# Narrower first scores and last weighed keys in the attention of a streaming-encoder block

## The chip, the cores and the metric

The kernel runs on one core of a Trainium2 chip. The metric is the device time of one execution in microseconds. TensorE is called PE here, its weight loads PEld, VectorE DVE, ScalarE ACT, GpSimd POOL, and SyncE, which issues most loads, SP.

## The reference, cut to what matters

One layer works on 512 frames of 1024 features. Most of its work is projections; the change is in the attention, with 16 heads of 64 features.

```python
xn = rmsnorm(h, norm_mix_g[l])
u = jnp.einsum('bsd,de->bse', xn, w_in[l])
q, k, v, xr, gr, ga, gb = jnp.split(u, splits, axis=-1)
ya = chunked_band_attention(q, k, v, rel_table[l]) @ w_attn_out[l]
...                       # recurrent branch yb, gates g_a and g_b
h = h + (g_a * ya + g_b * yb) @ w_o[l]
...                       # SwiGLU feed-forward, final norm
# in the attention: chunks of 64 frames, each sees its own chunk and 8 before it
s = jnp.einsum('bnqhd,bnkhd->bhnqk', q, kb).astype(jnp.float32) * scale
s = s + rel_bias_band(rel_table)
s = jnp.where(valid, s, NEG_INF)
p = jax.nn.softmax(s, axis=-1)
o = jnp.einsum('bhnqk,bnkhd->bnqhd', p, vb)
```

With 512 frames there are 8 chunks, so a frame sees every key up to the end of its own chunk: the scores are block-triangular.

## The kernel before, in words

All products run on PE with operands of the type fp32r, a 32-bit type that carries fewer bits of the mantissa. To reach fp32 accuracy each operand is split into a high part and a low rest: ACT copies a tile to fp32r (line 80) and DVE subtracts that from the original (line 81). A projection then multiplies three times for each block of 128 features (lines 74 to 76: high by high, high by low, low by high).

The stages follow each other: norm and recurrent branch with its projections, attention, the output projections, the feed-forward block. The attention stage lies in the profile from about 235 to 449 us. For each head:

- `scores(h)` makes four score tiles, one for each block `qb` of 128 queries. Block `qb` needs the first `(qb + 1) * 128` keys. The matmul's stationary operand is a block of q, the moving operand the keys `kh` and then `kl` (lines 624 and 625). The tiles of `qb` 0, 1 and 3 share two PSUM buffers with the tag `s`; that of `qb` 2 takes one of the four `mm` buffers. DVE adds the bias and finds the maximum (627), ACT makes the exponential and its row sum (628), DVE takes the reciprocal of the sums (629), POOL scales (631).
- `transposed(h, prob)` turns the ten 128x128 blocks on PE into three PSUM tiles (643), and each is split into `pp[0]`, `pp[1]`, `pp[2]`. The third holds key block 2 (two query blocks) and key block 3 (one).
- `weigh(h, pp)` multiplies with v into one PSUM tile `o` (663): key block by key block, high and low. The halves of the result are then summed by ACT (664) and DVE (665) into `oacc`.

Both places that the change touches work with at least 256 columns in the moving operand. Query block 0 computes 256 key columns of which 128 are read. Key block 3 is weighed with 256 columns, the first 128 of which POOL has filled with zeros (637), so that the third tile has a gap at columns 256 to 383, and its split is made in two pieces.

Between the heads the projections of q and k for the next pair of heads, of v, and of the gate run as fill: a list of steps of which `fill` takes some before and some after each weighing. `k_tile` copies the high part of k twice (584 and 586), subtracts on DVE (585), and POOL copies the rest (587); the scores of a new pair's first head need these. The order of instructions on each engine is not the program's own: a scheduler of the framework (`schedule_with_timeline_sim=True`) places all instructions by its model of their costs, so a change of one operation can move others. Each engine works through its instructions in the order so made.

## Time and profile before

| what | value |
|---|---|
| median of three runs | 892.38 us (891.75 to 892.43) |
| the profiled execution | 892.82 us |
| its span in the profile | 891.0 us |
| granted PE clock | 0.996 of full speed |
| PE busy | 875.7 us, 98% |
| DVE, ACT, POOL busy | 553.5, 473.2, 130.2 us |

The rows that follow have a start, a length, an engine, a source line, an operation and the tiles as "output<-inputs", with the sizes of the operands. In a group's row the count stands behind an x, then the busy time, the mean of one in ns, the idle time of the engine just before these instructions, and what ended that idle time. Matmuls overlap and their ends are modelled, so the cost of a matmul is read from the distance of two starts and not from its length.

### The profile page before, as it was taken

To read this page: it belongs to the slowest core of one execution; us is meant where nothing else is said; L and a number is where in the kernel's file an instruction comes from. 1 tells how busy PE (TensorE), PEld (TensorE's weight loads), DVE (VectorE), ACT (ScalarE), POOL (GpSimd) and SP (SyncE) were. 2 spreads that over 40 slices of the span, in tenths; PEclk is the share of its full clock that TensorE was granted. 3 is DMA by queue.
4 is the path that set the end of the run, shared out by engine and by line. 5 is a ranking of instruction groups with operands and counts; after the bars stand their busy time and mean duration, and the time that the engine had idled before them with its cause. 6 is when DMAs were issued, how large, how long until landed. Compare 5 with 4: busy or idle time off the path is not lost.

```text
span 891.0 us, 13319 instructions
## 1 busy us (share of the span) xinstructions
PE 875.7 (98%) x5220; PEld 779.4 (87%) x5220; DVE 553.5 (62%) x863; ACT 473.2 (53%) x841; POOL 130.2 (15%) x168
## 2 busy tenths in 40 slices
PE   8999999999999999999999999899999999999997
PEld 5988888888889889898888889899999999888886
DVE  5777557563466675666456356998788887463203
ACT  7566646652266676667434366556655556723203
POOL 4012112120022222323000003400000001300200
PEclk9999999999999999999999999899999999999999
DMA  8323223333332232331224430333333333253102
GB/s 264 89 79 111 82 91 95 120 95 95 106 104 74 77 101 72 94 96 61 71 85 145 172 95 25 95 119 116 122 95 95 97 115 101 97 187 125 37 1 96
DMA packets 85024, 89.06 MB, mean 100 GB/s; under 512 B 5344, under 2 KB 73552, under 8 KB 84960
## 3 DMA queue, kind: packets, MB, share of 16 engines
q1 hardware_dynamic: 83584, 84.73, 30.7%
q10 hardware_dynamic: 1376, 3.47, 1.0%
q8 instruction: 41, 0.67, 0.3%
q14 instruction: 23, 0.19, 0.1%
HBM read 86.05 MB, written 2.14 MB: 99 GB/s over the span
## 4 chain that ended last, share of the span: by engine, by line
PE 94%; DVE 3%; ACT 1%; issue 1%; DMA 1%; POOL 0%; SPq 0%; ACTq 0%
PE po_out L74 5%; PE po_out L76 5%; PE po_out L75 5%; PE p_fu L75 2%; PE p_fu L74 2%; PE o L663 2%; PE p_fu L76 2%; PE p_fg L75 2%; PE p_fg L76 2%; PE p_fg L74 2%; PE pT L643 2%; PE po_v L76 2%; PE po_v L75 2%; PE po_v L74 2%; PE po_q L74 2%; PE q_fg L76 2%
## 5 line engine op out<-in xcount | busy, mean ns | idle before, releaser
L75 PE MATMUL po_out<-whl_fo,act_hi 128*128 128x512 f32 (+1 forms) x198 | 72.4, 366 | 0.0
L74 PE MATMUL po_out<-whl_fo,act_hi 128*128 128x512 f32 (+1 forms) x198 | 72.4, 366 | 0.0
L76 PE MATMUL po_out<-whl_fo,act_lo 128*128 128x512 f32 (+1 forms) x198 | 71.6, 365 | 0.0
L631 POOL TENSOR_SCALAR p<-p,rl 128x128 f32<-128x128 f32 (+1 forms) x64 | 35.9, 583 | 142.0 <-DVE rl L629 142.0
L81 DVE TENSOR_TENSOR whl_fo<-raw_fo,whl_fo 128x1024 fp32r<-128x1024 f32 x22 | 27.6, 1261 | 45.5 <-ACT whl_fo L80 45.1
L80 ACT ACTIVATE whl_fo<-raw_fo 128x1024 fp32r<-128x1024 f32 x22 | 22.9, 1056 | 49.3 <-PE po_out L76 35.0
L627 DVE CUSTOM_DVE_ANT_0 p<-s,bias 128x384 f32<-128x384 f32 (+2 forms) x64 | 29.5, 484 | 21.5 <-PE s L625 20.9
L76 PEld LDWEIGHTS po_out<-whl_fo,act_lo 128*128 128x128 f32 x198 | 37.3, 189 | 6.0
L75 PEld LDWEIGHTS po_out<-whl_fo,act_hi 128*128 128x128 f32 x198 | 37.4, 189 | 6.0
L74 PEld LDWEIGHTS po_out<-whl_fo,act_hi 128*128 128x128 f32 x198 | 37.4, 189 | 6.0
L628 ACT ACTIVATE p<-p,m 128x384 f32<-128x384 f32 (+2 forms) x64 | 35.7, 560 | 12.6 <-DVE m L627 12.2
L843 POOL TENSOR_TENSOR act_lo<-act,act_hi 128x1024 fp32r<-128x1024 f32 x4 | 10.5, 2621 | 185.9 <-ACT act_hi L842 184.4
L76 PE MATMUL po_v<-whl_v,xnT 128*128 128x256 f32 x128 | 36.2, 283 | 0.0
L75 PE MATMUL po_v<-whl_v,xnT 128*128 128x256 f32 x128 | 36.1, 282 | 0.0
L74 PE MATMUL po_v<-whl_v,xnT 128*128 128x256 f32 x128 | 36.1, 282 | 0.0
L81 DVE TENSOR_TENSOR pp<-pT,pp 128x512 fp32r<-128x512 f32 (+1 forms) x64 | 29.3, 484 | 5.3 <-ACT pp L80 5.0
L81 DVE TENSOR_TENSOR whl_fu_s<-s_fu,whl_fu_s 128x1024 fp32r<-128x1024 f32 x20 | 25.3, 1280 | 5.8 <-ACT whl_fu_s L80 5.7
L75 PE MATMUL po_xr<-xnT,whl_xr 128*128 128x512 f32 (+1 forms) x80 | 27.9, 354 | 0.6 <-DVE xnT L331 0.6
L74 PE MATMUL po_gr<-xnT,whl_gr 128*128 128x512 f32 (+1 forms) x80 | 27.8, 349 | 0.1
L76 PE MATMUL po_gr<-xnT,whl_gr 128*128 128x512 f32 (+1 forms) x80 | 27.5, 348 | 0.3 <-DVE whl_gr L81 0.3
L75 PE MATMUL po_gr<-xnT,whl_gr 128*128 128x512 f32 (+1 forms) x80 | 27.6, 346 | 0.0
L74 PE MATMUL po_xr<-xnT,whl_xr 128*128 128x512 f32 (+1 forms) x80 | 26.6, 351 | 0.8 <-ACT xnT L330 0.8
(354 smaller groups left out, 3077.1 us busy)
## 6 DMA issues: line engine op xcount, KB each, us to landing
raw_fg<-in_w_ffn_in_dram SPq DMA_DIRECT2D x22, 512.0 KB, 4.4
raw_fu<-in_w_ffn_in_dram SPq DMA_DIRECT2D x22, 512.0 KB, 3.5
raw_fo<-in_w_ffn_out_dram SPq DMA_DIRECT2D x22, 512.0 KB, 4.0
raw_qk<-in_w_in_dram SPq DMA_DIRECT2D x32, 256.0 KB, 3.2
raw_xr<-in_w_in_dram SPq DMA_DIRECT2D x8, 512.0 KB, 4.6
raw_gr<-in_w_in_dram SPq DMA_DIRECT2D x8, 512.0 KB, 3.5
raw_ga<-in_w_in_dram SPq DMA_DIRECT2D x8, 512.0 KB, 3.9
raw_gb<-in_w_in_dram SPq DMA_DIRECT2D x8, 512.0 KB, 3.5
```

Source lines behind the costliest of these rows:

```text
L74: pe.matmul(o, sh, mh, start=start, stop=False, skip_group_check=parts)
L75: pe.matmul(o, sh, ml, start=False, stop=False, skip_group_check=parts)
L76: pe.matmul(o, sl, mh, start=False, stop=stop, skip_group_check=parts)
L80: act.activation(hi, src, AF.Copy)
L81: dve.tensor_sub(lo, src, f(hi))
L627: dve.tensor_tensor_reduce(prob[qb][:], sc[:, 0:w], bias[:, S - w:S], -1.0, 3e38, ALU.add, ALU.min, nmax[:, qb:qb + 1])
L628: act.activation(prob[qb][:], prob[qb][:], AF.Exp, bias=nmax[:, qb:qb + 1], scale=-1.0, accum_out=lsum[:, qb:qb + 1])
L631: pool.tensor_scalar(prob[qb][:], prob[qb][:], rl[:, qb:qb + 1], 1.0, ALU.mult, ALU.mult)
L643: pe.transpose(pt[:, at * P:(at + 1) * P], prob[qb][:, kb * P:(kb + 1) * P], ident[:])
L663: pe.matmul(po[:, S - n:S], st, pp[i][:, part, lo:lo + n], start=kb == 0 and part == 0, stop=kb == NT - 1 and part == 1)
L843: (pool if i in (0, 1, 2, 4) else dve).tensor_sub(lo[:], o[:], f(hi[:]))
```

## The change

Three edits, all in the attention.

- The scores of query block 0 are made for 128 key columns, where there were 256. The other blocks keep their widths.
- The third transpose tile is split in one piece of 384 columns, so key block 3 now lies at columns 256 to 383 of `pp[2]`; the gap, and POOL's zero fill of it, go.
- Key block 3 is weighed with 128 columns into the last 128 columns of `o`, where there were 256 into the last 256.

The third transposes stay in a bank of the four `mm` buffers, as they are before.

```diff
         for qb in range(NT):
             w = (qb + 1) * P
-            wm = max(w, 256)
...
-            pe.matmul(sc[:, 0:wm], qs, kh[:, e, 0:wm], start=True, stop=False)
-            pe.matmul(sc[:, 0:wm], qs, kl[:, e, 0:wm], start=False, stop=True)
+            pe.matmul(sc[:, 0:w], qs, kh[:, e, 0:w], start=True, stop=False)
+            pe.matmul(sc[:, 0:w], qs, kl[:, e, 0:w], start=False, stop=True)
...
         pp = [aw2.tile([P, 2, S], F32R, tag="pt", bufs=4, name=f"pp{h}_{i}") for i in range(3)]
-        pool.memset(f(pp[2][:, :, 256:384]), 0.0)
...
-            for at, lo, n in (((0, 0, 512),), ((0, 0, 384),), ((0, 0, 256), (384, 256, 128)))[i]:
-                split(pp[i][:, 0, at:at + n], pp[i][:, 1, at:at + n], pt[:, lo:lo + n])
+            n = (512, 384, 384)[i]
+            split(pp[i][:, 0, 0:n], pp[i][:, 1, 0:n], pt[:, 0:n])
...
-            i, lo, n = ((0, 0, 512), (1, 0, 384), (2, 0, 256), (2, 256, 256))[kb]
+            i, lo, n = ((0, 0, 512), (1, 0, 384), (2, 0, 256), (2, 256, 128))[kb]
```

In the changed kernel the lines from 624 on carry numbers that are one lower, and from 638 on two lower.

## The prediction

> **What bounds the kernel now.** I read the page first, then the stretches of the attention stage, then PE's own timeline there, then the order in which the built instructions of both kernels stand on each engine.

> ```profile
> span 891.0 us, 13319 instructions
> PE 875.7 (98%) x5220; PEld 779.4 (87%) x5220; DVE 553.5 (62%) x863; ACT 473.2 (53%) x841; POOL 130.2 (15%) x168
> ...
> PE 94%; DVE 3%; ACT 1%; issue 1%; DMA 1%; POOL 0%; SPq 0%; ACTq 0%
> ...
> 300.00:325.00 25.00, 24.51 (x126) 20.80 (x125) 16.02 (x34) 16.28 (x35) 7.23 (x14) 1.00 0.32 86
> ```

> PE is busy for 98% of the span and makes 94% of the chain that ended last. The last row is one stretch of the attention stage (length, then busy time of PE, weight loads, DVE, ACT, POOL, granted clock 1.00): PE has half a microsecond free in 25, the others a third of their time or more. So only two things can move the time: what a PE instruction costs, and how long PE waits. Work taken from ACT, DVE and POOL counts only through waits of PE.

> **What a matmul costs.** Starts of neighbouring matmuls and weight loads give the pace.

> ```profile
> 235.83 0.28 PE L624 MATMUL s<-kh,q 128*128 128x256 f32 x1
> 235.95 0.28 PE L625 MATMUL s<-kl,q 128*128 128x256 f32 x1
> 236.07 0.34 PE L624 MATMUL s<-kh,q 128*128 128x384 f32 x1
> 236.25 0.34 PE L625 MATMUL s<-kl,q 128*128 128x384 f32 x1
> 236.42 0.39 PE L74 MATMUL po_yb<-rnn,whl_yb 128*128 128x512 f32 x1
> 236.65 0.40 PE L75 MATMUL po_yb<-rnn,whl_yb 128*128 128x512 f32 x1
> ...
> 9.72 0.30 PEld L74 LDWEIGHTS po_xr<-xnT,whl_xr 128*128 128x128 f32 x2 [0.65 <-ACT xnT L330]
> 10.27 0.19 PEld L75 LDWEIGHTS po_xr<-xnT,whl_xr 128*128 128x128 f32 x1 [0.25 <-DVE xnT L331]
> 10.38 0.19 PEld L76 LDWEIGHTS po_xr<-xnT,whl_xr 128*128 128x128 f32 x1
> ...
> 302.97 1.09 PE pT L643 x10
> ```

> The next matmul starts 0.12 us after one of 256 columns, 0.17 to 0.18 after 384, 0.23 after 512: about 0.053 for each 128 columns, and 0.012 on top. A matmul of 128 columns would by that line take 0.053 + 0.012, some 0.065. But every one of these matmuls brings its own weights. Two loads that follow each other after a pause, with no full matmul between them to set the pace, stand 0.11 apart (10.27 and 10.38; and two in 0.30 where one takes 0.19). I read 0.11 as the least distance of two loads, so a narrow matmul can hardly pass in less. The only matmuls of 128 columns in this stage, the transposes, also go at 0.109 each (10 in 1.09, from the chain).

> **The change part by part.** First, the narrowed matmuls.

> ```profile
> L624 PE MATMUL s<-kh,q 128*128 128x256 f32 x32 | 9.7, 325 | 2.0 <-ACT kh L586 2.0
> ...
> L625 PE MATMUL s<-kl,q 128*128 128x256 f32 x32 | 8.5, 294 | 0.0
> ...
> L663 PE MATMUL o<-pp,v 128*128 128x256 f32 x64 | 11.7, 281 | 0.0
> ```

> Half of each group is narrowed (block 0 of the two score blocks of that width, key block 3 of the two in the weighing): 16 + 16 + 32 = 64 matmuls. At 0.12 before and 0.11 after I take 0.01 each, **-0.6 us**. No row shows a product of this type with fewer than 256 columns, so both ends stay open: at 0.065 the 64 save 0.055 each, -3.5 us; if such a product needed four passes it would cost what 512 columns cost, 0.23, or +0.11 each, +7.0 us. I take 0.11 because the load rows and the transposes both lie there.

> [...]

> Second, what leaves the other engines: 16 zero fills on POOL, and one split in place of two for each third transpose tile.

> ```profile
> L637 POOL MEMSET pp<- 128x256 f32 x15 | 4.8, 318 | 8.3 <-PE o L663 7.6
> ...
> L80 ACT ACTIVATE pp<-pT 128x384 fp32r<-128x384 f32 x16 | 7.7, 482 | 0.0
> ...
> L80 ACT ACTIVATE pp<-pT 128x256 fp32r<-128x256 f32 x16 | 6.2, 386 | 0.0
> L80 ACT ACTIVATE pp<-pT 128x128 fp32r<-128x128 f32 x16 | 4.4, 275 | 1.5 <-DVE pp L81 1.3
> ```

> ACT has 386 + 275 - 482 = 179 ns less for each head, 2.9 us in all, DVE about as much, POOL some 5 us. PE's busy time hides all of that; I cost it at nothing by itself. If that cover were gone, at most 0.18 us per head, 2.9 us, could show as gain.

> Third, the order. A scheduler places the instructions, and 16 fewer operations make it place them anew. The built order of PE is nearly as before until head 4; then it differs in many places of the attention stage, and behind that stage it is the same again. SP only swaps a load with its neighbour twice; the weight copies that read such loads keep PE waiting nowhere in the rows here, so that is nothing. Most moves are neutral: a transpose or a weighing slipped into a projection. One is not, and it comes twice, at heads 6 and 14. Before, PE goes: all of the last k projection, 8 weighing matmuls of head 4, 10 transposes of head 5, then the first scores of head 6, which need the new k. These rows are that place:

> ```profile
> 309.96 0.39 PE L76 MATMUL po_k<-xnT,whl_qk 128*128 128x512 f32 x1
> 310.18 1.44 PE L663 MATMUL o<-pp,v 128*128 128x512 f32 x8
> 311.46 1.25 PE L643 MATMUL pT<-ident,p 128*128 128x128 f32 x10
> 313.21 0.68 PE L624 MATMUL s<-kh,q 128*128 128x256 f32 x3 [0.49 <-ACT kh L586]
> ...
> 310.38 0.59 ACT L584 ACTIVATE kh<-po_k 64x512 fp32r<-64x512 f32 x1 [1.60 <-PE po_k L76]
> 310.88 1.05 ACT L80 ACTIVATE whl_v<-raw_v 128x1024 fp32r<-128x1024 f32 x1
> 311.95 0.59 ACT L664 ACTIVATE oacc<-o 64x512 f32<-64x512 f32 x1
> 312.57 0.59 ACT L586 ACTIVATE kh<-po_k 64x512 fp32r<-64x512 f32 x1
> 313.18 0.59 ACT L584 ACTIVATE kh<-po_k 64x512 fp32r<-64x512 f32 x1
> ...
> 311.96 1.48 DVE L81 TENSOR_TENSOR whl_v<-raw_v,whl_v 128x1024 fp32r<-128x1024 f32 x1 [0.27 <-ACT whl_v L80]
> 313.36 0.67 DVE L665 TENSOR_TENSOR oacc<-o,oacc 64x512 f32<-64x512 f32 x1
> 314.07 0.70 DVE L585 TENSOR_TENSOR kl<-po_k,kh 64x512 fp32r<-64x512 f32 x1
> ...
> L628 ACT ACTIVATE p<-p,m 128x512 f32<-128x512 f32 x16 | 11.6, 724 | 10.0 <-DVE m L627 10.0
> ...
> L627 DVE CUSTOM_DVE_ANT_0 p<-s,bias 128x128 f32<-128x128 f32 x16 | 4.5, 283 | 2.2 <-PE s L625 1.8
> ```

> The scores wait for ACT's second copy of kh, which ends at 313.16. PE was done with its transposes at 311.46 + 1.09 = 312.55 and waits 0.66. In the changed order two things are otherwise. The last score block of head 5 stands inside the k projection, three matmuls from its end, so its exponential (724 ns; neighbours on ACT overlap by some 0.09, as 310.38 + 0.59 against 310.88 shows) falls between the weight copy at 310.88 and the oacc copy: the kh copy ends 0.63 later, at 313.8. And the scores stand ahead of the ten transposes, so PE is at them at 310.18 + 1.28 = 311.46 and waits until 313.84, with the 1.09 of transposes still to do. That is 0.63 + 1.09 = 1.72 us lost each time.

> Behind it follows a second wait. After two score blocks and three transposes (0.46 + 0.33, to 314.63) PE wants the 512-column block of head 6, whose PSUM buffer is free when DVE has read block 0. On DVE that read stands behind the second kl subtraction, which needs the fifth row of ACT: that copy follows the kh copy from 313.8 to 314.4, then 0.70 and 0.28 on DVE, to about 315.4. PE waits 0.77. Queued behind it are the rest of head 5's transposes and the next projection. Together 2.5 us each time, **+5.0 us** for two. Bounds: 1.1 each (the exponential finds a gap on ACT and the buffer comes free in time, so only the 1.09 of transposes is lost) to 2.6 (a restart costs 0.1 more), so 2.2 to 5.2.

> Fourth, a gain at the end of the stage.

> ```profile
> PEld pT L643 <- POOL p L631: 0.7, 2, 0.4
> ```

> These two waits of the last head's transposes for POOL's scaling have more projection ahead of the chain they wait for in the new order, and POOL is 5 us lighter: I take **-0.7**, bounds 0 and -0.7.

> Sum: 5.0 - 0.6 - 0.7 = **+3.7 us**. The profiled execution took 892.82 with a span of 891.0, so 1.8 lie around the span; the median of the three runs is 892.38, 0.4 less. On the median I forecast 892.4 + 3.7 = **896.1 us**. No change can be told below 0.2%, 1.8 us, either way.

> **Rivals.** (1) Four passes: the narrow products cost as much as 512 columns, +7.0 instead of -0.6. The narrow weighings just ahead of the two long waits would be hidden in them (four times 0.11, 0.4 us): 892.4 + 5.0 + 7.0 - 0.4 - 0.7 = 903.3. For it speaks only that no narrow product of this type is in the trace; against it the transposes, also 32-bit, at 0.109. (2) Streaming pace: narrow products at 0.065, -3.5: 892.4 + 5.0 - 3.5 - 0.7 = 893.2, no change to be told. Against it speak the loads 0.11 apart. [...] (3) The new waits do not come: ACT runs ahead at heads 6 and 14 so that the waits stay what they were: 892.4 - 0.6 - 0.7 = 891.1. Against it: nothing lies between 310.38 and 313.16 on ACT but its own work, and one more operation stands in that row. (4) Faster: loads overlap more than the rows show, narrow products go at 0.065, and the freed 0.18 us per head on ACT covers the new waits: 892.4 - 3.5 - 0.7 = 888.2. It decides where the narrow interval is under 0.10 (64 times 0.02 and the 0.7 make 1.9) and the waits at both places stay at what they are now.

> **How the numbers follow.** My forecast has 0.70, with a range of its own from 893.3 (waits at 2.2) to 897.6 (waits at 5.2, the two gains at nothing). Four passes 0.11, streaming pace 0.09, no new waits 0.04, faster 0.06. From 891.0 to 898.2 the range takes the forecast with some room for restart costs, and rivals 2 and 3; rivals 1 and 4 and a tail of 0.02 are left out. Slower by over 0.2%: 0.68 of the forecast and 0.11, 0.79. Within: 0.09 + 0.04 + 0.02 = 0.15. Faster: 0.06.

> **What would show it.** In PE's timeline after, narrow scores and weighings follow each other by 0.11; 0.065 or 0.23 would prove rival 2 or 1. In the waits, scores on ACT's kh come four times as now, but two of them with some 2.4 us, and new waits of scores on DVE's read of p, two with some 0.8. If PE's idle time in the stage from the first scores to the last weighing does not grow by 4 to 5 us, the third step is wrong, whatever the total.

## The result: 1% slower, two and a half times what was forecast

| | us |
|---|---|
| before, median of 4 | 892.15 |
| the changed kernel, median of 4 | 901.31 (899.84 to 902.49) |
| ratio, 95% interval | 1.0102 (1.0083 to 1.0122) |
| forecast, range | 896.1 (891.0 to 898.2) |

The change costs 9.2 us, where +3.7 was forecast, and lies outside the range. The sign and the two places are as forecast; the size is not. The profiled execution of the changed kernel took 899.84, 7.0 more than that of before (892.82), and was the shortest of the four.

From the page of the changed kernel, its span and the first two engines:

```profile
span 898.1 us, 13316 instructions
PE 876.3 (98%) x5220; PEld 779.8 (87%) x5220; DVE 554.0 (62%) x847; ACT 472.5 (53%) x825; POOL 123.5 (14%) x152
```

PE still has 98% of the span, and its busy time hardly moved (875.7 before), so the loss must be sought in single stretches. The next view cuts the trace at the two places that the prediction named. Columns: stretch, length, then busy time (and count) of PE, weight loads, DVE, ACT, POOL, then the granted clock, the DMA share and GB/s. First the changed kernel, then before:

```profile
308.00:326.00 18.00, 14.02 (x67) 11.55 (x66) 9.67 (x24) 9.40 (x22) 5.63 (x12) 0.91 0.34 88
408.00:426.00 18.00, 14.98 (x68) 12.39 (x67) 10.35 (x25) 10.61 (x24) 5.49 (x11) 0.91 0.23 73
426.00:500.00 74.00, 74.00 (x348) 61.89 (x347) 41.77 (x60) 30.05 (x45) 2.06 (x4) 1.00 0.30 102
```

```profile
308.00:326.00 18.00, 17.51 (x90) 14.83 (x89) 11.78 (x24) 12.10 (x24) 7.23 (x14) 1.00 0.33 88
408.00:426.00 18.00, 17.50 (x95) 14.93 (x94) 10.19 (x21) 11.67 (x24) 5.55 (x11) 1.00 0.20 61
426.00:500.00 74.00, 73.79 (x338) 61.12 (x337) 41.35 (x60) 29.29 (x46) 2.05 (x4) 1.00 0.39 135
```

Two things changed in each place. PE's idle time went from 0.49 to 3.98 and from 0.50 to 3.02 us: 6.0 more in all. And the granted clock, 1.00 before, is 0.91 over 18 us. The second was in no step of the prediction and in no rival. (The granted clock is the share of the full clock that PE was given; 0.50 is half clock.)

PE's timeline at head 6 in the changed kernel (start, length, line, tiles; in brackets the idle time ahead and what ended it):

```profile
309.43 0.39 PE L76 MATMUL po_k<-xnT,whl_qk 128*128 128x512 f32 x1
309.66 1.37 PE L661 MATMUL o<-pp,v 128*128 128x512 f32 x8
313.38 0.50 PE L623 MATMUL s<-kh,q 128*128 128x128 f32 x2 [2.36 <-ACT kh L586]
313.72 0.39 PE L624 MATMUL s<-kl,q 128*128 128x128 f32 x2
315.73 1.14 PE L641 MATMUL pT<-ident,p 128*128 128x128 f32 x3 [1.62 <-POOL p L630]
316.52 0.78 PE L623 MATMUL s<-kh,q 128*128 128x512 f32 x1
```

The weighings come at once behind the k projection; then PE waits 2.36 us for ACT's second copy of kh, makes four short score matmuls, and waits a second time, 1.62 us, for POOL. At head 14 the same two waits take 2.36 and 0.53. What follows is stretched: from the first of three transposes to the next start it is 0.79, 0.26 each, where the prediction's rows had 0.109. The chain of copies on ACT there:

```profile
309.86 0.59 ACT L584 ACTIVATE kh<-po_k 64x512 fp32r<-64x512 f32 x1 [2.11 <-PE po_k L76]
310.35 1.05 ACT L80 ACTIVATE whl_v<-raw_v 128x1024 fp32r<-128x1024 f32 x1
311.30 0.71 ACT L627 ACTIVATE p<-p,m 128x512 f32<-128x512 f32 x1
312.12 0.59 ACT L662 ACTIVATE oacc<-o 64x512 f32<-64x512 f32 x1
312.74 0.59 ACT L586 ACTIVATE kh<-po_k 64x512 fp32r<-64x512 f32 x1
```

The exponential at 311.30 stands between the weight copy and the oacc copy, as the prediction read from the built order, and the kh copy ends at 313.33. So the first wait has the cause that was forecast; its rise, from 0.49 to 2.36, is 1.87 where 1.72 was forecast. The second is not: the forecast had 0.77 us for DVE's read of a score tile. What POOL did, and where the reciprocal on DVE and the bias load on SP's queue stood:

```profile
315.06 0.15 POOL L398 MEMSET bias<- 64x64 f32 x1 [3.22 <-DVE m L626]
315.30 2.06 POOL L630 TENSOR_SCALAR p<-p,rl 128x128 f32<-128x128 f32 x4
```

```profile
312.84 0.16 DVE L628 RECIPROCAL rl<-l 128x4 f32<-128x4 f32 x1
```

```profile
310.05 0.44 SPq L397 DMA_DIRECT2D bias<-ext_d  x1
```

The reciprocal that POOL's scaling of p needs was ready at 313.0. But the small fill that cuts the bias mask of the next head stands ahead of the scaling in POOL's queue, and it needs the bias load issued at 310.05. It ran at 315.06, 4.6 us after that issue was over, and the scaling at 315.30, 2.3 us later than it could have. (The fill's row names DVE, which ended an instruction at 315.01; by the trace's semaphores the fill waits for the load alone, whose last piece landed at 315.01 too.) The load was late for the same reason as the kh copy: its buffer is the one that the last scores of head 5 read, and these now stand inside the k projection. Before, that load was issued at 306.98.

Then the clock. These are stretches of 3.41 us in the changed kernel that end or begin where the clock was switched:

```profile
312.04:315.45 3.41, 0.72 (x4) 0.53 (x4) 2.88 (x8) 2.58 (x6) 0.30 (x2) 1.00 0.73 178
315.45:318.87 3.42, 3.14 (x11) 2.57 (x12) 0.70 (x2) 1.04 (x5) 2.52 (x5) 0.50 0.21 63
318.87:322.28 3.41, 3.41 (x16) 2.74 (x15) 0.74 (x3) 1.22 (x4) 1.53 (x4) 1.00 0.28 72
414.44:417.85 3.41, 1.05 (x5) 0.67 (x5) 2.97 (x7) 2.58 (x6) 1.18 (x4) 1.00 0.55 176
417.85:421.26 3.41, 3.29 (x11) 2.90 (x12) 1.50 (x7) 2.01 (x7) 1.90 (x4) 0.50 0.26 93
```

In the stretch from 312.04 PE was busy for 0.72 of 3.41 us; the whole next stretch is at clock 0.50, and the one after at 1.00. The same at 414.44 (busy 1.05). The trace has the half-clock stretches at 315.45 and 417.85, 102.40 us apart, which is 30 times 3.413. At clock 0.50 the 512-column matmul of the scores at 317.10 is followed after 0.42, where the pace is 0.23 at clock 1.00 (L74 to L76 from 319.54). As an estimate, 3.14 and 3.29 us of PE's busy time at clock 0.50 make half of the work: 1.6 lost each time, 3.2 in all.

The sum from the first scores to the first matmul of the stage behind attention (po_h): 250.68 us before (235.60 to 486.28), 258.60 after (235.50 to 494.10), so +7.9. Idle time over the whole stretch rose by 5.9 (the 6.0, 0.2 less at 426 to 500, and 0.1 elsewhere), half clock makes 3.2, and -1.2 is left for the narrow matmuls and the rest.

That the profiles differ by 7.0 and not by 7.9 comes from behind the stage, which is 0.8 shorter (403.95 us against 404.75): before has half clock there too, for 6.83 us from 562.39, the changed kernel for 3.41 from 571.45. So half clock is not new in the changed kernel; at heads 6 and 14 it is.

The narrow matmuls, first scores of the stage:

```profile
235.50 0.22 PE L623 MATMUL s<-kh,q 128*128 128x128 f32 x1
235.55 0.28 PE L624 MATMUL s<-kl,q 128*128 128x128 f32 x1
235.67 0.33 PE L623 MATMUL s<-kh,q 128*128 128x256 f32 x1
235.84 0.28 PE L624 MATMUL s<-kl,q 128*128 128x256 f32 x1
```

The first narrow one is followed after 0.05, the second after 0.12, so none is slow. What the first gains is given back behind it: the 256-column matmul at 235.67 is followed after 0.17, not 0.12. Three starts take 0.34, and three of 256 columns took 0.35 before (235.60 to 235.95): the weight loads, at 235.50, 235.61 and 235.72, stand 0.11 apart and set the pace of the group.

### The profile page after: what moved, and what is told of

It reads as the page before. It is cut to its first block, busy times and chain, and to the rows that moved or that the text cites. A ratio compares the mean times of both kernels' runs of the same rounds, so it can differ in the third digit from the quotient of the medians.

```text
span 898.1 us, 13316 instructions
## 1 busy us (share of the span) xinstructions
PE 876.3 (98%) x5220; PEld 779.8 (87%) x5220; DVE 554.0 (62%) x847; ACT 472.5 (53%) x825; POOL 123.5 (14%) x152
## 4 chain that ended last, share of the span: by engine, by line
PE 93%; DVE 2%; ACT 1%; issue 1%; SPq 1%; DMA 1%; POOL 0%; POOLq 0%; DVEq 0%; ACTq 0%
PE po_out L75 4%; PE po_out L74 4%; PE po_out L76 4%; PE p_fu L76 2%; PE p_fu L75 2%; PE p_fu L74 2%; PE p_fg L76 2%; PE p_fg L74 2%; PE p_fg L75 2%; PE pT L641 2%; PE o L661 2%; PE po_v L74 2%; PE po_v L76 2%; PE po_v L75 2%; PE po_ga L74 2%; PE po_q L74 2%
## 5 line engine op out<-in xcount | busy, mean ns | idle before, releaser
L75 PE MATMUL po_out<-whl_fo,act_hi 128*128 128x512 f32 (+1 forms) x198 | 72.4, 366 | 0.0
L74 PE MATMUL po_out<-whl_fo,act_hi 128*128 128x512 f32 (+1 forms) x198 | 72.4, 366 | 0.0
L76 PE MATMUL po_out<-whl_fo,act_lo 128*128 128x512 f32 (+1 forms) x198 | 71.6, 365 | 0.0
L81 DVE TENSOR_TENSOR whl_fo<-raw_fo,whl_fo 128x1024 fp32r<-128x1024 f32 x22 | 27.6, 1262 | 45.5 <-ACT whl_fo L80 45.0
L630 POOL TENSOR_SCALAR p<-p,rl 128x128 f32<-128x128 f32 (+1 forms) x64 | 34.0, 551 | 116.3 <-DVE rl L628 111.0
L80 ACT ACTIVATE whl_fo<-raw_fo 128x1024 fp32r<-128x1024 f32 x22 | 23.0, 1057 | 49.3 <-PE po_out L76 34.9
L626 DVE CUSTOM_DVE_ANT_0 p<-s,bias 128x128 f32<-128x128 f32 (+2 forms) x64 | 30.1, 488 | 22.2 <-PE s L624 21.6
L627 ACT ACTIVATE p<-p,m 128x128 f32<-128x128 f32 (+2 forms) x64 | 35.7, 559 | 14.7 <-DVE m L626 13.7
L74 PEld LDWEIGHTS po_out<-whl_fo,act_hi 128*128 128x128 f32 x198 | 37.4, 189 | 6.1
L76 PEld LDWEIGHTS po_out<-whl_fo,act_lo 128*128 128x128 f32 x198 | 37.3, 189 | 6.1
L75 PEld LDWEIGHTS po_out<-whl_fo,act_hi 128*128 128x128 f32 x198 | 37.4, 189 | 5.9
L74 PE MATMUL po_v<-whl_v,xnT 128*128 128x256 f32 x128 | 36.6, 286 | 0.0
L76 PE MATMUL po_v<-whl_v,xnT 128*128 128x256 f32 x128 | 36.2, 283 | 0.0
L75 PE MATMUL po_v<-whl_v,xnT 128*128 128x256 f32 x128 | 36.2, 283 | 0.0
L841 POOL TENSOR_TENSOR act_lo<-act,act_hi 128x1024 fp32r<-128x1024 f32 x4 | 10.5, 2621 | 185.6 <-ACT act_hi L840 184.1
L81 DVE TENSOR_TENSOR pp<-pT,pp 128x384 fp32r<-128x384 f32 (+1 forms) x48 | 26.8, 596 | 10.5 <-ACT pp L80 10.4
L81 DVE TENSOR_TENSOR whl_fu_s<-s_fu,whl_fu_s 128x1024 fp32r<-128x1024 f32 x20 | 25.3, 1279 | 5.8 <-ACT whl_fu_s L80 5.7
L75 PE MATMUL po_xr<-xnT,whl_xr 128*128 128x512 f32 (+1 forms) x80 | 27.9, 354 | 0.6 <-DVE xnT L331 0.6
L74 PE MATMUL po_gr<-xnT,whl_gr 128*128 128x512 f32 (+1 forms) x80 | 27.8, 349 | 0.1
L81 DVE TENSOR_TENSOR whl_qk<-raw_qk,whl_qk 128x1024 fp32r<-128x1024 f32 x16 | 19.7, 1230 | 13.3 <-ACT whl_qk L80 13.3
L76 PE MATMUL po_gr<-xnT,whl_gr 128*128 128x512 f32 (+1 forms) x80 | 27.5, 348 | 0.3 <-DVE whl_gr L81 0.3
L75 PE MATMUL po_gr<-xnT,whl_gr 128*128 128x512 f32 (+1 forms) x80 | 27.6, 346 | 0.0
```

Of the source, the lines that this page charges most:

```text
L74: pe.matmul(o, sh, mh, start=start, stop=False, skip_group_check=parts)
L75: pe.matmul(o, sh, ml, start=False, stop=False, skip_group_check=parts)
L76: pe.matmul(o, sl, mh, start=False, stop=stop, skip_group_check=parts)
L80: act.activation(hi, src, AF.Copy)
L81: dve.tensor_sub(lo, src, f(hi))
L626: dve.tensor_tensor_reduce(prob[qb][:], sc[:, 0:w], bias[:, S - w:S], -1.0, 3e38, ALU.add, ALU.min, nmax[:, qb:qb + 1])
```

## The experiments

The theory after this reading: the one-piece split changes the order that the scheduler builds; the order makes PE wait twice at heads 6 and 14; and the idle time costs a stretch of half clock behind each place. Rivals: the narrow matmuls or the missing fill cost time in a way the rows hide; the one-piece split itself does; the idle time alone is the loss and the clock only a companion.

| kernel | median us | ratio to before, 95% interval |
|---|---|---|
| scores only | 891.29 | 0.9991 (0.9982 to 0.9999) |
| change without narrow scores | 900.58 | 1.0090 (1.0076 to 1.0103) |
| two-piece split | 891.66 | 0.9994 (0.9985 to 1.0003) |
| added matmuls in the wait | 898.56 | 1.0071 (1.0058 to 1.0084) |
| one piece at head 2 only | 898.43 | 1.0065 (1.0051 to 1.0079) |
| one piece at four heads | 892.04 | 0.9995 (0.9986 to 1.0004) |
| mask on DVE | 899.76 | 1.0078 (1.0065 to 1.0090) |
| kh copies first | 893.99 | 1.0021 (1.0012 to 1.0030) |
| kh late by one copy | 895.59 | 1.0039 (1.0026 to 1.0051) |
| kh late by three copies | 900.82 | 1.0097 (1.0083 to 1.0111) |
| added matmuls, mask on DVE | 898.00 | 1.0071 (1.0058 to 1.0085) |
| weight copies on POOL | 908.00 | 1.0181 (1.0167 to 1.0195) |

Before was measured beside each group of runs, at 892.43 to 892.45.

**Scores only.** Before, with this and nothing else:

```diff
-            wm = max(w, 256)
+            wm = w
```

> Only the scores are narrowed (32 matmuls of 128 columns); fill, two splits and wide last weighing stay as before, and the built order of PE, ACT, DVE and POOL is that of before. If loads set the pace (0.11 us each, as the changed kernel's trace shows) the gain is 32 x 0.01 = 0.3 us, no change to be told, no wait of PE over 1 us in heads 6 and 14, granted clock 1.00 there. If narrow products were the cost (four passes) it would be 32 x 0.11 = 3.5 us slower, half of it if the cost lies in the scores' share of the change; if they streamed at 0.065, 1.8 us faster.

Measured 0.8 us under before by the ratio (0.1 to 1.6). Four passes are ruled out; a gain of 1.8 lies just outside the interval.

**The change without the narrow scores.** The changed kernel, with 256 columns for the first scores again:

```diff
-            pe.matmul(sc[:, 0:w], qs, kh[:, e, 0:w], start=True, stop=False)
+            pe.matmul(sc[:, 0:max(w, 256)], qs, kh[:, e, 0:max(w, 256)], start=True, stop=False)
```

and the same for kl.

> The change without the narrow scores: no fill, one third split, last key block 128 wide; the built order is that of the changed kernel on every engine. Order theory: the two long waits at heads 6 and 14 and the half clock behind them are all there, so some 9 us slower than before (8 to 10.5), as the changed kernel. If the narrow scores had a part in the loss, visibly less than that, by 3.5 us at four passes.

Measured 900.58: nearly the whole loss without the narrow scores. They have no part in it that could be told.

**Two-piece split.** Both narrowings, no fill, the layout of the change, but:

```diff
-            n = (512, 384, 384)[i]
-            split(pp[i][:, 0, 0:n], pp[i][:, 1, 0:n], pt[:, 0:n])
+            for lo, n in (((0, 512),), ((0, 384),), ((0, 256), (256, 128)))[i]:
+                split(pp[i][:, 0, lo:lo + n], pp[i][:, 1, lo:lo + n], pt[:, lo:lo + n])
```

> The changed kernel with both narrowings and no fill, but the third split done in two pieces (256 and 128 columns) as before; the built order of PE is then that of before but for a few neighbours. Order theory: no long wait at heads 6 and 14, clock 1.00 there, and only the narrow matmuls' gain is left: 64 x 0.01, so 891.0 to 892, the same as before or up to 1.4 us faster. If narrow products or the missing fill made the loss, it stays some 9 us slower.

Measured 891.66. All 64 narrow matmuls and no fill, and no loss; so of the three edits only the one-piece split carries it. From the first scores to po_h it takes 250.28 us, 0.4 less than before. The waits for kh are back to the 2.0 us of before, from 5.8 in the changed kernel (us in all, times, longest):

```profile
PE s L623 <- ACT kh L586: 2.1, 4, 0.5
```

**Added matmuls in the wait.** The changed kernel, and ahead of the scores of heads 6 and 14:

```diff
+            if h in (6, 14) and qb == 0:
+                for _ in range(8):
+                    pe.matmul(sc[:], xnT[0][:, 0, 0:P], xnT[0][:, 0, :], start=True, stop=True)
```

> The changed kernel with eight added matmuls of 512 columns, whose product is overwritten by the first scores, in heads 6 and 14: one stands ahead of the weighings there and seven between these and the first scores, so they run in the 2.36 us in which PE otherwise waits for ACT's copy of kh (7 x 0.23 = 1.6 us). They shorten no wait. Clock theory (PE's idle time brings the granted clock to half for 3.4 us behind each wait, which costs about 1.7 us each): clock stays at 1.00 there, and the time comes to 896 to 898, 3 to 4 us below the changed kernel with 16 matmuls more. Rival (the time is lost in the waits alone): half clock or not, no gain, or a loss of up to 2 x 0.23 + 0.4 us, so 901 to 902.

Measured 898.56 (897.17 to 900.54), 2.75 under the changed kernel though PE has sixteen matmuls more to do, and a little above the 896 to 898 expected. PE's timeline at the first place and the stretches of both:

```profile
311.13 1.83 PE L625 MATMUL s<-xnT 128*128 128x512 f32 x7
313.42 0.49 PE L626 MATMUL s<-kh,q 128*128 128x128 f32 x2 [0.46 <-ACT kh L586]
```

```profile
308.00:326.00 18.00, 16.09 (x81) 13.07 (x80) 10.51 (x26) 10.51 (x25) 5.63 (x12) 1.00 0.33 88
408.00:426.00 18.00, 16.64 (x84) 13.54 (x83) 10.10 (x25) 10.97 (x25) 5.48 (x11) 1.00 0.23 74
```

The wait for kh shrinks to 0.46 because it is filled, the scores start at the same time as in the changed kernel (313.42 against 313.38) and the clock is 1.00 at both places. From the first scores to po_h the profile takes 255.83 us, 2.8 less than the changed kernel's. Work that computes nothing made the kernel faster: that part of the loss was clock. The profile is of the fastest of five runs that spread over 3.4 us; its mean clock is 0.999, that of the others 0.993 to 0.995, so half-clock stretches are left in those, at places that no trace shows.

**One piece at head 2 only, and at four heads.** The two-piece kernel, with one condition at that split:

```diff
-            for lo, n in (((0, 512),), ((0, 384),), ((0, 256), (256, 128)))[i]:
+            for lo, n in (((0, 512),), ((0, 384),), ((0, 256), (256, 128)) if h != 2 else ((0, 384),))[i]:
```

> Both narrowings and no fill as in the change, the third split in two pieces for 15 of the 16 heads and in one only for head 2. In the built order that one operation less is enough to give PE, ACT and POOL the changed kernel's order around head 6, and there alone: around head 14 it is that of before. Order theory: one place with some 4 us of waits and the half clock behind it, so half of the changed kernel's loss: +4.7 us on the two-split kernel's 891.7, that is 895 to 897. If the loss belonged to the one-piece splits themselves, one of 16 would cost 0.6 us.

Measured 898.43. The second kernel has another condition, four heads in one piece:

```diff
- if h != 2 else
+ if h % 8 not in (4, 5) else
```

> The same with the third split in one piece for four heads (4, 5, 12 and 13, those that are weighed and transposed just at the two places), in two for the others; the built order keeps that of before around heads 6 and 14. Order theory: no long wait, clock 1.00 there, the two-split kernel's time: 891 to 892.3. If the one-piece split itself were the loss, a quarter of it (2.3 us) or, as it stands at the two places, all of it: 894 to 901.

Measured 892.04. The two places in the first of them, and POOL's fill there:

```profile
308.00:326.00 18.00, 13.56 (x59) 11.04 (x58) 8.73 (x20) 8.26 (x19) 5.61 (x12) 0.81 0.35 88
408.00:426.00 18.00, 17.47 (x92) 14.88 (x90) 12.94 (x30) 13.17 (x30) 4.38 (x7) 1.00 0.23 74
```

```profile
315.54 0.15 POOL L398 MEMSET bias<- 64x64 f32 x1 [3.70 <-DMA bias<-ext_d]
315.78 2.05 POOL L630 TENSOR_SCALAR p<-p,rl 128x128 f32<-128x128 f32 x4
```

One piece at one head of sixteen costs 6.8 us, at a place four heads further on; one piece at four heads, those at the two places among them, costs 0.4, which is within what can be told. So the one-piece split is innocent in itself, and the order that follows from it is the cause. The forecast of half the loss (895 to 897) was low: this profile has 4.4 us of idle time and two half-clock stretches in a row at head 6 (0.81 over 18 us), none at head 14. The row of POOL's fill names the bias load as what it waited for.

**Mask on DVE.** The changed kernel, at line 398:

```diff
-        pool.memset(b[64:128, 448:512], NEG)
+        dve.memset(b[64:128, 448:512], NEG)
```

> The changed kernel, with the small fill that cuts the bias mask (64 x 64, behind the bias load) on DVE instead of POOL; the order on PE around heads 6 and 14 is the changed kernel's but that six of the ten transposes follow the first scores at once. Queue theory of the second wait (POOL stood at the mask until the bias load landed, and the scaling of p behind it, which the transposes wait for, came 2 us late): the 2.4 us wait for kh stays, the 1.6 us wait for POOL goes or falls under 0.6, 2 x 1.0 to 1.6 us less than the changed kernel's 900 to 901.5, and up to 2 x 1.7 more where the clock keeps at 1.00: 895 to 899. Rival (the transposes wait for the exponentials and the reciprocal, not for the mask): 900 to 902 as before, the wait still 1.6.

Measured 899.76. What POOL and PE did, and the stretches of 3.41 us:

```profile
314.34 2.05 POOL L630 TENSOR_SCALAR p<-p,rl 128x128 f32<-128x128 f32 x4 [1.36 <-DVE rl L628]
```

```profile
314.46 0.50 PE L623 MATMUL s<-kh,q 128*128 128x128 f32 x2 [2.35 <-ACT kh L586]
315.03 1.65 PE L641 MATMUL pT<-ident,p 128*128 128x128 f32 x6
317.74 0.79 PE L623 MATMUL s<-kh,q 128*128 128x512 f32 x1 [0.42 <-DVE m L626]
```

```profile
311.71:315.12 3.41, 1.06 (x9) 0.87 (x8) 2.17 (x3) 3.24 (x6) 1.38 (x3) 1.00 0.81 197
315.12:318.53 3.41, 2.99 (x11) 2.01 (x10) 2.61 (x9) 1.14 (x4) 1.88 (x4) 0.50 0.55 157
318.53:321.95 3.42, 3.42 (x10) 2.65 (x9) 0.88 (x3) 1.74 (x6) 0.89 (x3) 0.50 0.25 60
```

POOL scales right behind the reciprocal, and the wait for POOL is gone, so the queue was its cause. But only 1.6 us came back; that is 0.8 above the upper end of the 895 to 899 expected. The fill now blocks DVE, which waits for the bias load and gives PE a wait of 0.42, and the one wait of 2.35 was enough: PE was busy for 1.06 in the stretch from 311.71, and two half-clock stretches follow. Over the whole stage PE is idle for 6.20 us where the changed kernel has 8.07, but three half-clock stretches stand against two. The profiled execution (900.18, mean clock 0.989) is one of the longer ones; two of the five took 897.7 and 897.9 at a mean clock of 0.993.

**kh late by one copy, by three.** The two-piece kernel with the order of before, where ACT repeats the second copy of kh at heads 6 and 14:

```diff
-            act.activation(kh[other, e], po[own, :], AF.Copy)
+            for _ in range(2 if pr in (3, 7) and e == 0 else 1):
+                act.activation(kh[other, e], po[own, :], AF.Copy)
```

The second kernel has `range(4 if` there.

> The two-split kernel (891.7) with ACT's second copy of kh done twice over for the k projections of heads 6 and 14 (one more copy of the same values). In the built order the copy that the scores wait for then stands behind three copies of transposes as well, while the ten transposes stay ahead of the scores: one wait of PE at each place, about 2.1 us (0.5 before), and none for POOL behind it. It prices one wait without the changed order. If a wait costs its length alone: 2 x 1.6 = 3.2, so 894.9. If 2 us of idle PE are enough to halve the clock for 3.4 us: 1.7 more at each place, 898.3.

> The same with three more copies, so one wait of about 3.3 us at each place. By its length alone 2 x 2.8 = 5.6, so 897.3. With the half clock 900.7 or more. If e9 keeps the clock at 1.00 and this one does not, the idle time from which the clock falls lies between 2.1 and 3.3 us.

Measured 895.59 and 900.82. First the wait and the 3.41 us stretches of the one, then of the other:

```profile
315.48 0.33 PE L624 MATMUL s<-kh,q 128*128 128x128 f32 x1 [2.42 <-ACT kh L587]
```

```profile
311.38:314.79 3.41, 1.68 (x15) 1.44 (x13) 3.13 (x4) 3.34 (x6) 1.09 (x3) 1.00 0.52 154
314.79:318.21 3.42, 2.73 (x14) 2.42 (x15) 3.13 (x11) 3.12 (x10) 0.62 (x1) 1.00 0.55 158
```

```profile
316.10 0.33 PE L624 MATMUL s<-kh,q 128*128 128x128 f32 x1 [3.66 <-ACT kh L587]
```

```profile
313.69:317.10 3.41, 1.00 (x7) 1.00 (x8) 1.99 (x7) 3.27 (x8) 0.00 (x0) 1.00 0.54 154
317.10:320.51 3.41, 3.41 (x10) 2.63 (x9) 1.61 (x6) 2.10 (x7) 0.62 (x1) 0.50 0.02 5
```

The wait of 2.42 costs its length: two times 2.42 - 0.5 is 3.8, measured 3.9 over the two-piece kernel. (By the trace it is 3.5 from the first scores to po_h, 253.80 against 250.28; the first scores themselves start 0.8 later in this profiled execution, at 236.22 against 235.40.) The wait of 3.66 costs more: two times 3.16 is 6.3, measured 9.2; the rest, 2.9, is put down to the half clock behind each place (the rows show the first), 3.41 us at a loss of up to 1.7 by the estimate that half of the work is lost. The changed order is not in these kernels. So the theory's third link is shown alone: behind the wait of 3.66 us came clock 0.50 without the changed order. The 2.42 us lay across two stretches here (busy 1.68 and 2.73, both at clock 1.00), while the 2.35 of the kernel before this fell into one (busy 1.06).

**Both edits together.** The changed kernel with the diff of the added matmuls and that of the mask on DVE.

> Both earlier edits on the changed kernel: eight added (overwritten) matmuls of 512 columns in the wait for kh, and the bias mask cut on DVE. Left idle at each place: some 0.5 for kh and 0.4 for DVE. If waits and half clock are the whole loss: clock 1.00, and from the 898.6 of the added matmuls alone the 1.3 us wait for POOL goes and 0.4 comes, twice: 896.8, in every run (no spread of 3 us). If something else of the changed order costs time, it stays at 898 to 899.

Measured 898.00, not 896.8, and the spread stayed (897.13 to 899.85). From its waits of PE:

```profile
PE s L626 <- DVE m L629: 1.8, 2, 1.4
```

The fill on DVE costs PE 1.4 us at one place: the wait for the bias load was moved from one queue to another. The clock was 1.00 at both places in the profile. That every run would be free of the spread was wrong. The mean clock of the five runs falls from 0.997 to 0.993 in the order of their times, so the longer ones had more half clock; at which places stays open.

**Two tries for a faster kernel.** In the two-piece kernel ACT makes both copies of kh ahead of the subtraction, against the four waits of 0.5 us that are left:

```diff
+            act.activation(kh[other, e], po[own, :], AF.Copy)
             dve.tensor_sub(kl[own, e], po[own, :], f(kh[own, e]))
-            act.activation(kh[other, e], po[own, :], AF.Copy)
```

> The two-split kernel (both narrowings, no fill, order of before), and in the k projection's epilogue both copies of kh on ACT issued ahead of the first subtraction for kl. A candidate to beat both: the four waits of the first scores for ACT's second kh copy (0.5 us each, with some 0.1 behind) go, 4 x 0.6 = 2.4 us, so 889.3. Rival: ACT's copy of oacc is pushed behind those copies, and the next q projection waits for that PSUM buffer some 1.1 us four times in place of the 0.6: 893.5.

Measured 893.99: the rival was right. Its waits of PE:

```profile
PE po_q L74 <- DVE oacc L663: 3.0, 3, 1.0
PE po_ga L74 <- DVE oacc L663: 1.0, 1, 1.0
```

The second try moves four weight copies from ACT to POOL:

```diff
+                elif name in ("v1", "v2", "v3", "ga4") and k == 4:
+                    pool.tensor_copy(hl[:, 0], raw[:])
+                    dve.tensor_sub(hl[:, 1], raw[:], f(hl[:, 0]))
```

> The two-split kernel with four weight copies (the second halves of v1, v2, v3 and ga4, 128 x 1024, those ahead of kh on ACT) on POOL instead of ACT. A candidate to beat both: ACT's second copy of kh then ends some 1.05 us sooner at the four places and the waits of 0.5 us for it go, with about 0.1 behind: 4 x 0.6 = 2.4 us off 891.7, so 889.3. Rival: POOL's copy is slow enough (over 2 us) to hold its copy of kl, which the second halves of the scores wait for: 891.7 or more.

Measured 908.00, 16 us slower, and for neither of the reasons given. Its waits of PE:

```profile
PE s L626 <- ACT kh L589: 7.2, 7, 2.0
PE pT L644 <- POOL p L633: 2.0, 2, 1.6
```

The scheduler built a pattern like the changed kernel's again, scores that wait 2.03 us for kh with the transposes behind them, at three places (clock 0.50 from 281.69 and from 336.30, behind stretches with PE busy for 0.89 and 1.37 of 3.41 us; 0.94 over 326 to 408, with PE idle for 4.77 of 82 us). Places against time over the two-piece kernel: none 0, one 6.8, two 9.6, three 16.3.

No version beats before by what a measurement can tell (0.2%); scores only is the nearest.

## Why the prediction failed where it did

- **Narrow matmuls, -0.6: right in the sum, in part by luck.** The two-piece kernel, which has all 64 and nearly the order of before, is 0.5 us under before by the ratio (1.3 under to 0.3 over) and 0.4 by the trace. Rivals 1 and 2 are wrong. The price of 0.01 each is not what the trace has: the first of two narrow ones passes in 0.05 to 0.06, the second in 0.11. From each start to the next, at clock 1.00 and without PE's idle time, the scores and weighings that had 256 columns before take 0.118 in the mean in the changed kernel, against 0.136 before: some 2.3 us over the 128 of them, or 0.04 for each of the 64 that were narrowed. A part of it is given back: a projection's 512-column matmul right behind a narrow weighing takes 0.28 there (8 of them), and took 0.236 behind a weighing of 256 columns before (14). The two-piece kernel, with the same narrow matmuls, keeps 0.4 in the net.
- **The other engines at nothing: right.** The missing fill and the shorter splits cost and gave nothing in themselves (two-piece split, one piece at four heads).
- **The order, first wait: right.** It rose by 1.87 at each place against 1.72 forecast, with the same exponential in the same row of ACT. Reading the built order gave the sign, and rivals 3 and 4, in which the waits stay as before, fell with it.
- **The order, second wait: wrong cause, and undersized.** The prediction followed the score tile to DVE (0.77 each, 1.5 in two). PE stood earlier, at the transposes of the head before, for POOL's scaling, by the waits of the changed kernel 2.2 us in two:

```profile
PE pT L641 <- POOL p L630: 2.2, 2, 1.6
```

  The prediction had looked at PE, ACT and DVE in the new order but passed over POOL, where a fill that needs a load stands ahead of the scaling. Idle time at the two places rose by 6.0 where 5.0 was forecast.
- **End of the stage, -0.7: mostly wrong.** The row that it was read from is of weight loads (PEld), which overlap matmuls; PE's own idle time from 426 to 500 was 0.21. It fell to nothing, so 0.2 came back.
- **The clock: missing.** This is the failed step that put the time out of the range: the sum costed a wait at its length alone and had half clock at nothing, and the profile has 3.2 us of it by the estimate above. Without these the median would be some 898.1, just inside the range. In the trace of the changed kernel each half-clock stretch at the two places is 3.41 us long, and the two lie a whole number of such lengths apart (the 102.40 above). The stretch before need not be idle throughout: one with PE busy for 1.05 us was followed by half clock, and so was, with the mask on DVE, one with PE busy for 1.06 and a single wait of 2.35.

Of the 4.2 us missing by the trace from the first scores to po_h (7.9 against 3.7), 3.2 are clock, 1.0 longer waits, 0.5 the gain at the end that did not come and 0.1 idle time elsewhere, less 0.6 that the remainder is better than forecast. The median lies 1.5 above the profiled execution; the four runs' mean clock goes from 0.989 to 0.993, but not in the order of their times, so what the other three lost beyond the profile stays open. One of the runs shows what it may be: the change without the narrow scores, with nearly the same waits (5.8 us for kh in four, 2.4 for POOL in two), was profiled at 901.08; 1.2 more than the changed kernel's 899.84, and half clock lasts 6.82 us from 313.31, twice as long as in the changed kernel's profile.

## What to carry to other kernels

Where a scheduler builds the order, removing an operation can cost time far from where it stood (here four heads further on): compare the built order on every engine, and follow each wait into all queues, GpSimd's small fills that stand behind a load among them. Where TensorE is the bound, look at the granted clock behind a wait before it is costed by its length. Here a wait of 2.42 us cost its length, with PE busy for 1.68 and 2.73 of the two stretches of 3.41 us that it lay across; waits that left PE busy for 0.72 to 1.37 of such a stretch were followed by clock 0.50 for one or two stretches, at up to 1.7 us more for each by the estimate that half of the work is lost.

## What the hardware showed

Stretches at clock 1.00 that were followed by one at clock 0.50:

| kernel | start of the stretch, us | PE busy, us |
|---|---|---|
| before | 558.98 | 0.99 |
| the changed kernel | 312.04, 414.44, 568.04 | 0.72, 1.05, 1.05 |
| change without narrow scores | 309.90 | 1.22 |
| one piece at head 2 only | 310.96 | 0.81 |
| mask on DVE | 311.71 | 1.06 |
| kh late by three copies | 313.69, 416.09 | 1.00, 0.88 |
| weight copies on POOL | 278.28, 332.89 | 0.89, 1.37 |

Stretches with more that were followed by clock 1.00 are those of 2.40 and 2.88 in the changed kernel (308.63, 411.02), of 1.68 with kh late by one copy (311.38), and of 2.16 with kh late by three (310.27). For busy times between 1.37 and 1.68 there is no row here.

Half-clock stretches with PE busy for 1.57 us (one piece at head 2 only), 1.82 (change without narrow scores), 2.32 (weight copies on POOL), 2.69 (before, 562.39) and 2.99 (mask on DVE) were followed by a second one. Those of 3.14, 3.29 and 3.41 us in the changed kernel (315.45, 417.85, 571.45) were the last.

Half clock is not of the attention alone. Between 500 and 600 us the granted clock is 1.00 throughout in the profile of the added matmuls; in each of the other thirteen, before among them, some part of that time has 0.93 to 0.98 in the mean (0.97 over the 100 us before, 0.98 in the changed kernel).
